# A pool of its own for the map's chunks, and six more places for gathered rows instead of four

## The chip, the cores and the metric

One core of one Trainium2 chip runs the whole program. The time is device microseconds (us) of one execution; shown are the median and the extremes of several. Everything is float32 in and out.

## The reference, cut to what matters

The kernel computes one decoder layer for 512 tokens of width 1024: mixing (attention and retention), then the expert retrieval `peer`, then a gate and a norm. The change concerns `peer`. Each token picks 8 x 16 = 128 of 16,384 experts; an expert is one row of `u` and one row of `v` (1024 floats each):

```
def peer(m, w_query, sub_keys, u, v):
    ...
    expert = jnp.take_along_axis(cand_idx, top_pos, axis=-1)
    gates = jax.nn.softmax(top_s, axis=-1)
    ...
    def chunk(args):
        xt, e, g = args
        u_sel = jnp.take(u, e, axis=0)
        act = jax.nn.gelu(jnp.einsum('cd,ced->ce', xt, u_sel).astype(jnp.float32), approximate=False) * g
        v_sel = jnp.take(v, e, axis=0)
        return jnp.einsum('ce,ced->cd', act.astype(xt.dtype), v_sel)
```

## The kernel before

The 512 tokens are four blocks of 128. The kernel treats them in two ways.

**The dense way (blocks 0 to 2, 384 tokens).** Every one of the 128 chunks of 128 experts is multiplied for all these tokens. A "u unit" is the product of one chunk of `u` with the tokens (24 matmuls into `ps`, line 85), after which ScalarE applies gelu. A "v unit" multiplies the weighted activations with one chunk of `v` and adds into six accumulators (18 matmuls into `acc`, line 781). Each unit's weights come as a 512 KB load `wraw` on SyncE's queue (lines 713, 719; `RAW` = 4 buffers), ScalarE makes the high part `wh` (line 745) and VectorE the low part `wl` (line 761). For a v unit VectorE also multiplies in the map (`av`, line 751), ScalarE rounds it to `ah` (line 754) and VectorE makes `al` (line 763). The weights of the experts chosen by each token are the "map": VectorE, TensorE and ScalarE build it in groups of 32 tokens. The chunks 0 to 23 (`KEEP`) stay in SBUF in the tile `kept`, 24 x 384 x 4 = 36,864 bytes of each partition; the other 104 go through a buffer `gs` (104 x 32 x 4 = 13,312 bytes, two of them) to DRAM (`g_d<-gs`, line 1137) and come back as `gv<-g_d` (line 726).

**The sparse way (block 3, 128 tokens).** For each of the 128 choices GpSimd gathers one row of `u` for each token, then one of `v`: 256 gathers of 128 rows x 4 KB (line 847, tile `row`). VectorE consumes each in a `sparse_step`: a dot product for `u` (line 858), a multiply-add into `yacc` for `v` (line 860). A gather can start only when its place is free, that is when the sparse step that read the place before is done. The pool `late` has three such places (`ROWS`). `gather()` is called after each sparse step and issues as many gathers as places are noted in `due`; a place of the pool `more` is given back only while `extra` is not empty.

**The order.** Each engine executes in the order in which the program writes its instructions. A first loop (lines 1183 to 1220) runs u units beside the building of the map. A second loop (lines 1370 to 1414) runs the rest of the u units, all v units and the last weights; it spreads the sparse steps by a table of costs. Sparse steps stand in VectorE's order between the instructions that make `wl` and `al`, so VectorE, waiting for a gathered row, also keeps back the operands of TensorE.

**The places in SBUF.** On the right side of SBUF pools open and close as a stack. `gsp` holds `kept` and the two `gs`. In the second loop `open_more` closes `gsp` and opens `more`, with `MORE` = 4 places, in its room; line 1391 allows that once the writes are issued (`not writes`) and the last unit that reads `kept` has been prepared (`prepared > last_kept`). 64 units before the end `open_fin` closes `more` and opens `fin`, the tiles of the last stage (`hs`, `pl`, `gl`, `gate_b`, `final_gain`), which SyncE's queue then loads.

Of the kernel before, what the change touches and what calls it, by code (L numbers as in the profile page):

```python
# [23 lines left out]
F32 = mybir.dt.float32  # L24
# [11 lines left out]
P = 128  # L36
# [4 lines left out]
ND = NT * P  # L41
# [13 lines left out]
def block_kernel(ctx: ExitStack, tc, t):  # L55
    nc = tc.nc

    def pool(name, bufs=1, **kw):
        return tc.tile_pool(name=name, bufs=bufs, reuse_waits="tile", **kw)
# [47 lines left out]
    def row_const(pool, name):  # L107

        r = pool.tile([P, D], F32, name=name)
        nc.sync.dma_start(r, row_src(name))  # L110
        return r
# [33 lines left out]
    with pool("wa", 2, side="right") as wa, pool("sm", 2, side="right") as sm, \  # L145
# [43 lines left out]
        def take():  # L189
            while steps[2] <= place[0]:  # L190
                cut_high()
                cut_low()
            place[0] += 1
            return cut_w.pop(place[0] - 1)
# [5 lines left out]
        def token_products(out, x, i):  # L200

            wh, wl = take()
            for k in range(2):
                xh, xl = x[2 * i + k]
                for b in range(4):
                    product3(out[b], [((xh[:, blk[b]], xl[:, blk[b]]), (wh[:, k], wl[:, k]))],
                             first=i + k == 0, last=i == 3 and k == 1)
            ahead()
# [4 lines left out]
        with pool("proj", side="right") as pj, pool("att", 2, side="right") as at:  # L213
# [276 lines left out]
            kept = []  # L490
# [202 lines left out]
        KEEP, RUN, QUAD = 24, 32, 4  # L693
# [12 lines left out]
        raw, parts, inputs, made, g_quad, kept_map = {}, {}, {}, {}, {}, []  # L706
# [107 lines left out]
        def spill(keep):  # L814

            while len(spills) > keep:
                nc.sync.dma_start(*spills.pop(0))

        vp, acc, count, done_u = [], [], [0], []
        writes, spills = [], []  # L820
# [12 lines left out]
        extra = {}  # L833
# [13 lines left out]
                nc.gpsimd.indirect_dma_start(out=rows[n], out_offset=None, in_=t[table],  # L847
                                             in_offset=bass.IndirectOffsetOnAxis(ap=e_sp[:, r:r + 1], axis=0))

        at_more, MORE = {}, 4  # L850

        def sparse_step():
            n = done[0]
# [13 lines left out]
        with pool("wp", 2, side="right") as wpp:  # L867
            hs = wpp.tile([P, 4, D], F32, name="hs", bufs=1)
            for b in range(4):
                nc.sync.dma_start(hs[:, b], t["x"][blk[b]])  # L870
            pT = wpp.tile([P, 2, S], F32, name="pT", bufs=1)
            nc.sync.dma_start(pT, t["pT"])
            gffn = row_const(wpp, "ffn_gain")
            ssm = sm.tile([P, 2, 4], F32, name="ssm", bufs=1)

            def add_mixing(half, ps):
                c = halves[half]
                for b in range(4):
                    nc.vector.tensor_tensor(hs[:, b, c], hs[:, b, c], ps[b], op=OP.add)
                    nc.scalar.activation(sqj[:, :S], hs[:, b, c], AF.Square, accum_out=ssm[:, half, b:b + 1])  # L880

            ps2 = [p.tile([P, S], F32, name="wo", tag=tag) for p, tag in ((psM, "misc"), (mm, "mm")) for _ in range(2)]
            token_products(ps2, cat, 0)
            add_mixing(0, ps)
            for i in range(1, 4):
                token_products(ps2, cat, i)
                if i == 1:
                    pH, pL = split(wpp, pT, [P, 2, S], "p", nc.vector, bufs=1)
                if i == 2:
                    for c in range(2):  # L890
                        load(("q", c))
                        prepare(("q", c), nc.vector)

            wh, wl = take()
            pp = [psS.tile([P, 2, S], F32, name="S", tag="S") for _ in range(2)]
            for b in range(4):
                product3(pp[b // 2][:, b % 2], [((pH[:, k, blk[b]], pL[:, k, blk[b]]), (wh[:, k], wl[:, k])) for k in range(2)])
            add_mixing(1, ps2)
            nc.sync.dma_start(h_d, hs)
            nc.vector.tensor_tensor(ssm[:, 0], ssm[:, 0], ssm[:, 1], op=OP.add)  # L900
            y = rstd(sm, ssm[:, 0], 4, D, 1e-6)
            mn = [wpp.tile([P, D], F32, name=f"mn{b}", bufs=1) for b in range(4)]
            for c in halves:
                for b in range(4):
                    if b % 2:
                        nc.vector.tensor_scalar(mn[b][:, c], hs[:, b, c], y[:, b:b + 1], None, op0=OP.mult)
                    else:
                        nc.scalar.activation(mn[b][:, c], hs[:, b, c], AF.Copy, scale=y[:, b:b + 1])
            mx = operand()
            for k in range(KC):  # L910
                pt = (psM, mm)[k % 2].tile([P, 4, P], F32, name="pt", tag=("misc", "mm")[k % 2])
                for b in range(4):
                    nc.tensor.transpose(pt[:, b], mn[b][:, k * P:(k + 1) * P], ident)
                scaled_split(*mx[k], pt.rearrange("p b t -> p (b t)"), gains[:, G_FFN, k:k + 1])
            kp = wpp.tile([P, 4, S], F32, name="kp", bufs=1)
            for b in range(2):
                nc.scalar.activation(kp[:, 2 * b:2 * b + 2], pp[b], AF.Copy)
            nc.sync.dma_start(ple_d[:, :, halves[1]], kp)
            nc.vector.tensor_tensor(mtok, mn[3], gffn, op=OP.mult)
    g_stack = ctx.enter_context(ExitStack())  # L920
    with pool("pk") as pk, pool("psG", 2, space=PSUM) as psG, pool("psT", space=PSUM) as psT:
        vals = pk.tile([P, 4, 16, TOPK], F32, name="vals")
# [20 lines left out]
        with pool("qs", 2) as qs:  # L943
            units = [("q", c) for c in range(16)] + [("u", n) for n in range(RAW - 1)]
            loaded, prepared = 2, 2
# [40 lines left out]
            rank(14)  # L986
            rank(15)

        gsp = g_stack.enter_context(pool("gsp", side="right"))
        kept_map.append(gsp.tile([P, KEEP, ND], F32, name="kept"))  # L990
        mh = pk.tile([P, ND], F16, name="mh")
        ml = pk.tile([P, ND], F16, name="ml")
        it = pk.tile([P, ND], BF16, name="it")
# [188 lines left out]
        n = 0  # L1182
# [50 lines left out]
    def open_fin():  # L1233

        extra.clear()
        while any(at_more.values()):
            sparse_step()
        more_stack.close()
        fin["p"] = fp = ctx.enter_context(pool("fin", 2, side="right"))
        for name, n in (("hs", 4), ("pl", 4)):  # L1240
            fin[name] = fp.tile([P, n, D], F32, name=name, bufs=1)
        fin["gl"] = fp.tile([P, KC, D], F32R, name="gl", bufs=1)
        for name in ("gate_b", "final_gain"):
            fin[name] = fp.tile([P, D], F32, name=name, bufs=1)
        fin["st"] = fp.tile([P, 8], F32, name="st", bufs=1)
# [66 lines left out]
    with pool("acc", space=PSUM) as pa:  # L1312
# [11 lines left out]
        n = 0  # L1324
# [19 lines left out]
        last_kept = max(n for n, u in enumerate(seq) if u[0] == "v" and u[1] < KEEP)  # L1344
# [3 lines left out]
        W_EVERY, END = 2, total - 64  # L1348
# [5 lines left out]
        writes = writes[2:]  # L1354
        prev = ("u", n_early - 1)
        loaded, prepared = RAW - 1, 2
# [13 lines left out]
        for n, u in enumerate(seq):  # L1370
            while loaded < min(total, n + RAW):
                kind, i = seq[loaded]
                if kind == "v" and i >= n_early and i not in late_a:
                    break
                assert kind != "v" or all((i - KEEP) // QUAD not in range(*x[1]) for x in writes)
                if kind == "g" and "gh" not in fin:
                    x = operand()
                    fin["gh"] = x
                load(seq[loaded])
                loaded += 1  # L1380
            while prepared < min(total, n + 3, loaded):
                prepare(seq[prepared], nc.vector)
                prepared += 1
            spill(0)
            finish(prev, prev[1] >= n_early)
            products(u)
            prev = u
            if writes and n % W_EVERY == 0:
                f, q, g = writes.pop(0)
                f(*q)  # L1390
            if not extra and n < END - 12 and not writes and prepared > last_kept:
                open_more()
            if n == END - 8:
                extra.clear()
            if n == END:
                open_fin()
            traffic += fixed[n]
            passed += busy_units[n]
            while done[0] < n_sp and (traffic + LOAD <= level * passed or n >= total - SPARSE_END):
                sparse_step()  # L1400
                gather()
                traffic += LOAD
            if 0 <= n - end_at < len(ends):
                name, b = ends[n - end_at]
                if b is None:
                    nc.sync.dma_start(fin[name], row_src(name))
                else:
                    nc.sync.dma_start(fin[name][:, b], sources[name][:, b])
            if n == total - 8:
                assert done[0] == n_sp  # L1410
                add_experts(3, [yacc[:, d * S:(d + 1) * S] for d in range(2)])
                fac[3] = rstd(fin["p"], fin["st"][:, 3:4], 1, D, 1e-6)
            if n == total - 2:
                turn(3, mm, "mm")
# [90 lines left out]
```

## Time and profile before

| | |
|---|---|
| median of 3 runs | 1603.94 us (1603.33 to 1609.25) |
| the profiled execution | 1605.48 us, of it span 1603.7 us |
| TensorE (PE) busy | 1542.4 us, 96% |
| VectorE (DVE) busy | 1222.3 us, 76% |
| ScalarE (ACT), GpSimd (POOL) busy | 678.9 us, 376.2 us |
| mean granted TensorE clock | 0.985 of full |
| moved by DMA | 402.72 MB, 251 GB/s on average |

TensorE is busy nearly all the time, so time can be found only where it stands still or runs slowly; the profile's table of stretches shows where. The page's chain of the work that ended last tells which wait holds TensorE up there. In the chain, "issue" is time in which an engine waited for nothing that the profile shows. The names of engines in the rows are PE (matmul), PEld (its weight load), DVE, ACT, POOL and SP.

### The profile page before, as it was taken

How to read it: one execution, taken by the hardware profiler on the slowest of the kernel's cores; microseconds unless marked ns; L12 is line 12 of the kernel's file. 1: busy time of each engine (PE TensorE's matmuls, PEld its weight loads, DVE VectorE, ACT ScalarE, POOL GpSimd, SP SyncE). 2: the span in 40 equal slices, each digit the busy share in tenths (PEclk: the TensorE clock that was granted, in tenths of full speed). 3: DMA queues.
4: the chain of work that ended last, by engine and by line, in shares of the span. 5: the costliest groups of instructions: out<-in, count | busy, mean ns of one | idle time of the engine just before them, and what ended most of it. 6: DMA issues, size and time to landing. Idle time of an engine off the chain costs nothing.

```text
span 1603.7 us, 22942 instructions
## 1 busy us (share of the span) xinstructions
PE 1542.4 (96%) x8209; PEld 1348.4 (84%) x8209; DVE 1222.3 (76%) x2523; ACT 678.9 (42%) x1077; POOL 376.2 (23%) x311
## 2 busy tenths in 40 slices
PE   8999999899999999999999898989999999999997
PEld 6787877787999999999999776777888888888885
DVE  3576565478998989998866787768888875897655
ACT  5455545444634453454343232323333333354444
POOL 1200000110013203203113444445434320432000
PEclk9899999999999999999999999999999999999998
DMA  6322324774458979987998888889999999899701
GB/s 230 102 76 79 112 99 185 213 176 117 167 187 268 319 219 316 297 283 259 315 295 305 307 301 306 308 288 343 408 386 366 359 328 346 302 401 345 255 28 48
DMA packets 163475, 402.72 MB, mean 251 GB/s; under 512 B 14528, under 2 KB 77259, under 8 KB 163233
## 3 DMA queue, kind: packets, MB, share of 16 engines
q1 hardware_dynamic: 123248, 256.06, 45.3%
q0 software_dynamic: 40112, 145.20, 27.2%
q8 instruction: 64, 1.05, 0.3%
q14 instruction: 51, 0.41, 0.1%
HBM read 350.61 MB, written 42.21 MB: 245 GB/s over the span
## 4 chain that ended last, share of the span: by engine, by line
PE 64%; DMA 13%; issue 11%; DVE 7%; POOL 2%; ACT 2%; SPq 0%; POOLq 0%; DVEq 0%; ACTq 0%
PE ps L85 32%; PE acc L781 19%; DMA row<-in_peer_v_dram,e_sp 7%; DMA row<-in_peer_u_dram,e_sp 4%; PE S L85 3%; POOL row L847 2%; PE S L322 1%; PE ps L517 1%; PE wo L85 1%; DVE wl L761 1%; PE pg L1116 1%; PE pg L1118 1%; DMA wraw<-in_u_t_dram 1%; PE sc L951 1%; DVE yacc L860 1%
## 5 line engine op out<-in xcount | busy, mean ns | idle before, releaser
L85 PE MATMUL ps<-xh,wh 128*128 128x384 f32 (+1 forms) x1312 | 466.4, 355 | 5.3 <-ACT kept L793 3.0
L85 PE MATMUL ps<-xh,wl 128*128 128x384 f32 (+1 forms) x1312 | 459.4, 350 | 7.3 <-DMA wl<-wraw 4.3
L85 PE MATMUL ps<-xl,wh 128*128 128x384 f32 (+1 forms) x1320 | 459.4, 348 | 0.0
L745 ACT ACTIVATE wh<-wraw 128x1024 fp32r<-128x1024 f32 x272 | 286.5, 1054 | 193.2 <-PE ps L85 101.8
L761 DVE TENSOR_TENSOR wl<-wraw,wh 128x1024 fp32r<-128x1024 f32 x258 | 314.6, 1221 | 64.7 <-ACT wh L745 60.0
L85 PEld LDWEIGHTS ps<-xh,wl 128*128 128x128 f32 x1312 | 248.6, 189 | 21.7 <-DMA wl<-wraw 4.8
L85 PEld LDWEIGHTS ps<-xh,wh 128*128 128x128 f32 x1312 | 249.1, 190 | 19.0 <-ACT kept L793 3.3
L847 POOL DMA_INDIRECT row<-in_peer_v_dram,e_sp x128 | 170.8, 1334 | 391.0 <-DVE act L858 309.6
L847 POOL DMA_INDIRECT row<-in_peer_u_dram,e_sp x128 | 169.1, 1321 | 387.4 <-DVE yacc L860 245.9
L85 PEld LDWEIGHTS ps<-xl,wh 128*128 128x128 f32 x1320 | 250.7, 190 | 10.7
L781 PE MATMUL acc<-wl,ah 128*128 128x512 f32 x768 | 240.2, 394 | 14.0 <-DVE wl L761 13.9
L781 PE MATMUL acc<-wh,ah 128*128 128x512 f32 x768 | 240.0, 394 | 9.6 <-ACT ah L754 9.4
L781 PE MATMUL acc<-wh,al 128*128 128x512 f32 x768 | 238.4, 392 | 0.0
L860 DVE SCALAR_TENSOR_TENSOR yacc<-row,act,yacc 128x1024 f32<-128x1024 f32 x128 | 163.9, 1280 | 30.6 <-DMA row<-in_peer_v_dram,e_sp 30.4
L781 PEld LDWEIGHTS acc<-wl,ah 128*128 128x128 f32 x768 | 143.8, 189 | 49.1 <-DVE wl L761 20.0
L858 DVE CUSTOM_DVE_ANT_0 junk<-row,mtok 128x1024 bf16<-128x1024 f32 x128 | 156.1, 1220 | 34.5 <-DMA row<-in_peer_u_dram,e_sp 34.1
L781 PEld LDWEIGHTS acc<-wh,ah 128*128 128x128 f32 x768 | 143.9, 189 | 44.4 <-ACT ah L754 15.6
L781 PEld LDWEIGHTS acc<-wh,al 128*128 128x128 f32 x768 | 143.8, 189 | 32.5 <-DVE al L763 3.2
L754 ACT ACTIVATE ah<-av 128x384 fp32r<-128x384 f32 x104 | 54.6, 525 | 255.0 <-PE acc L781 145.1
L1126 ACT ACTIVATE gs<-pg 128x832 f32<-128x832 f32 x48 | 41.5, 865 | 146.1 <-PE pg L1118 114.2
L763 DVE TENSOR_TENSOR al<-av,ah 128x384 fp32r<-128x384 f32 x104 | 57.7, 554 | 55.5 <-ACT ah L754 55.5
L185 DVE TENSOR_TENSOR wl<-wraw,wh 128x1024 fp32r<-128x1024 f32 x33 | 40.6, 1230 | 29.2 <-ACT wh L179 29.0
(288 smaller groups left out, 1711.6 us busy)
## 6 DMA issues: line engine op xcount, KB each, us to landing
wraw<-in_u_t_dram SPq DMA_DIRECT2D x128, 512.0 KB
wraw<-in_peer_v_dram SPq DMA_DIRECT2D x128, 512.0 KB
gv<-g_d SPq DMA_DIRECT2D x26, 768.0 KB
g_d<-gs SPq DMA_DIRECT2D x24, 576.0 KB
a<-av SPq DMA_DIRECT2D x72, 192.0 KB
av<-a SPq DMA_DIRECT2D x72, 192.0 KB
wraw<-in_w_in_t_dram SPq DMA_DIRECT2D x16, 512.0 KB
wraw<-in_wq_t_dram SPq DMA_DIRECT2D x16, 512.0 KB
```

Source lines behind the costliest of these rows:

```text
L85: nc.tensor.matmul(out, a, b, start=first and k == 0, stop=last and k == n - 1)
L185: nc.vector.tensor_tensor(cut_w[k][1], raw_w.pop(k), cut_w[k][0].bitcast(F32), op=OP.subtract)
L322: nc.tensor.matmul(out, *((a, b) if q_first else (b, a)), start=n == 0, stop=n == 1)
L745: nc.scalar.activation(wh, w, AF.Copy)
L754: nc.scalar.activation(ah, av, AF.Copy)
L761: low.tensor_tensor(wl, w, wh.bitcast(F32), op=OP.subtract)
L763: nc.vector.tensor_tensor(al, av, ah.bitcast(F32), op=OP.subtract)
L781: nc.tensor.matmul(acc[b][d], a[:, c], bb[:, d * S:(d + 1) * S], start=f, stop=l)
L847: nc.gpsimd.indirect_dma_start(out=rows[n], out_offset=None, in_=t[table], in_offset=bass.IndirectOffsetOnAxis(ap=e_sp[:, r:r + 1], axis=0))
L858: nc.vector.tensor_tensor_reduce(junk, row, mtok, 1.0, 0.0, OP.mult, OP.add, act[:, r:r + 1])
L860: nc.vector.scalar_tensor_tensor(yacc, row, act[:, r:r + 1], yacc, op0=OP.mult, op1=OP.add)
L1126: nc.scalar.activation(gs[0][:, :, t0:t0 + 8], pgi[:, KEEP:], AF.Copy, scale=2.0 ** -15)
```

## The change

`kept` moves from `gsp` into a pool of its own, opened just ahead of `gsp` on the same side. So `gsp` now holds only the two `gs`, and closing it no longer needs the readers of `kept` to be done. `open_more` may run as soon as no write is left to be issued; it opens 6 places (24,576 bytes) where the two `gs` (26,624 bytes) were. The pool of `kept` is closed in `open_fin`.

```
-        at_more, MORE = {}, 4
+        at_more, MORE = {}, 6
...
+    k_stack = ctx.enter_context(ExitStack())
     g_stack = ctx.enter_context(ExitStack())
...
+        kept_pool = k_stack.enter_context(pool("kept", side="right"))
+        kept_map.append(kept_pool.tile([P, KEEP, ND], F32, name="kept"))
         gsp = g_stack.enter_context(pool("gsp", side="right"))
-        kept_map.append(gsp.tile([P, KEEP, ND], F32, name="kept"))
...
         more_stack.close()
+        k_stack.close()
         fin["p"] = fp = ctx.enter_context(pool("fin", 2, side="right"))
...
-            if not extra and n < END - 12 and not writes and prepared > last_kept:
+            if not extra and n < END - 12 and not writes:
                 open_more()
```

On every engine the instructions stand in the same order as before; what differs is what some of them wait for. Numbering the gathers from 0, the first one into a place of `more` was gather 157; now it is gather 67. GpSimd's queue, with the semaphores that each gather waits for, before, from gather 65 on (`DMASW` counts GpSimd's transfers, `DMAHW` SyncE's, `DVE` and `Activation` those engines' instructions):

```order
L847 DMA row<-in_peer_v_dram,e_sp 128x1024 [waits DMASW0_49,DVE_49]
L847 DMA row<-in_peer_u_dram,e_sp 128x1024 [waits DMASW1_49,DVE_49]
L847 DMA row<-in_peer_v_dram,e_sp 128x1024 [waits DMASW2_49,DVE_49]
L847 DMA row<-in_peer_u_dram,e_sp 128x1024 [waits DMASW3_49,DVE_49]
L847 DMA row<-in_peer_v_dram,e_sp 128x1024 [waits DMASW4_49,DVE_49]
L847 DMA row<-in_peer_u_dram,e_sp 128x1024 [waits DMASW5_49,DVE_49]
L847 DMA row<-in_peer_v_dram,e_sp 128x1024 [waits DMASW6_49,DVE_49]
```

The same place now:

```order
L847 DMA row<-in_peer_v_dram,e_sp 128x1024 [waits DMASW0_49,DVE_49]
L847 DMA row<-in_peer_u_dram,e_sp 128x1024 [waits DMASW1_49,DVE_49]
L847 DMA row<-in_peer_v_dram,e_sp 128x1024 [waits DMAHW4_49,DMAHW3_49,DMAHW5_49,DMAHW2_49,DMAHW6_49,DMAHW1_49,DMAHW7_49,DMAHW0_49,Activation_49]
L847 DMA row<-in_peer_u_dram,e_sp 128x1024 [waits DMAHW5_49,DMAHW6_49,DMAHW4_49,DMAHW7_49,DMAHW3_49,Activation_49]
L847 DMA row<-in_peer_v_dram,e_sp 128x1024
L847 DMA row<-in_peer_u_dram,e_sp 128x1024
L847 DMA row<-in_peer_v_dram,e_sp 128x1024
L847 DMA row<-in_peer_u_dram,e_sp 128x1024 [waits DMASW2_49]
```

Gathers 67 and 68 wait for SyncE's transfers out of the two `gs` (and ScalarE's filling of them), gathers 69 to 72 for nothing that frees a place, and from gather 73 on each waits again for the sparse step that frees its place, which is now nine steps back instead of three.

A second place is SyncE's queue where `fin` opens. Before:

```order
L719 DMA wraw<-in_peer_v_dram 128x1024 [waits DMAHW4_49,DMAHW3_49,DVE_49]
L1408 DMA hs<-h_d 128x1024
L719 DMA wraw<-in_peer_v_dram 128x1024 [waits DMAHW7_49,DMAHW5_49,DVE_49]
L731 DMA av<-a_6497 128x384 [waits DMAHW6_49]
L1408 DMA hs<-h_d 128x1024
```

Now:

```order
L719 DMA wraw<-in_peer_v_dram 128x1024 [waits DMAHW4_49,DMAHW3_49,DVE_49]
L1411 DMA hs<-h_d 128x1024 [waits DMASW4_49,DMASW5_49,DMASW3_49,DMASW6_49,DMASW2_49,DMASW7_49,DMASW1_49,DMASW0_49]
L719 DMA wraw<-in_peer_v_dram 128x1024 [waits DMAHW7_49,DMAHW5_49,DVE_49]
L731 DMA av<-a_6500 128x384 [waits DMAHW6_49]
L1411 DMA hs<-h_d 128x1024
```

The first load of `hs` now waits for the gathers that used `more`, since `hs` lies partly where those places were; the loads of `final_gain` and `gate_b`, which waited for them before, no longer do.

## Rows read from the trace of the kernel before

**Rows 1.** Busy time of each engine by stretch: start:end, length, engines, clock, DMA share, GB/s

```profile
600.00:700.00 100.00, 100.00 (x733) 97.64 (x732) 91.88 (x179) 42.22 (x58) 26.74 (x20) 1.00 0.91 307
...
851.00:1110.00 259.00, 233.80 (x1069) 193.27 (x1068) 196.06 (x245) 80.03 (x113) 121.01 (x90) 0.99 0.86 307
1110.00:1160.00 50.00, 50.00 (x236) 44.03 (x237) 44.69 (x58) 17.35 (x23) 29.78 (x23) 0.97 1.00 392
1160.00:1290.00 130.00, 130.00 (x597) 110.47 (x597) 110.81 (x148) 47.64 (x66) 48.62 (x40) 1.00 0.97 366
...
1070.00:1080.00 10.00, 5.10 (x16) 3.82 (x15) 7.64 (x10) 2.63 (x5) 4.26 (x4) 0.83 0.73 257
```

**Rows 2.** The chain of waits, 840 to 1170 us: start, length, what

```profile
1063.51 9.71 DMA row<-in_peer_v_dram,e_sp
...
1077.61 4.39 DMA row<-in_peer_v_dram,e_sp
...
1109.84 30.02 PE acc L781 x124
1139.87 16.66 PE ps L85 x96
```

**Rows 3.** Who waited for whom, 851 to 1110 us: total us, times, longest

```profile
DVE junk L858 <- DMA row<-in_peer_u_dram,e_sp: 32.2, 22, 5.0
...
DVE yacc L860 <- DMA row<-in_peer_v_dram,e_sp: 26.0, 24, 3.2
PEld acc L781 <- DVE wl L761: 19.8, 20, 5.3
```

**Rows 4.** Stretches, matmuls into `acc` alone: length, busy (count), clock, DMA share, GB/s

```profile
851.00:1110.00 259.00, 170.10 (x705) 0.99 0.86 307
1110.00:1160.00 50.00, 33.50 (x140) 0.97 1.00 392
1160.00:1290.00 130.00, 113.50 (x501) 1.00 0.97 366
```

**Rows 5.** The same stretches, matmuls into `ps` alone

```profile
851.00:1110.00 259.00, 64.83 (x364) 0.99 0.86 307
1110.00:1160.00 50.00, 16.83 (x96) 0.97 1.00 392
1160.00:1290.00 130.00, 16.83 (x96) 1.00 0.97 366
```

**Rows 6.** GpSimd's queue in time: start, length, instruction, idle before and its releaser

```profile
851.01 0.94 POOL L847 DMA_INDIRECT row<-in_peer_v_dram,e_sp  x1 [23.78 <-DVE act L858]
...
1108.92 1.68 POOL L847 DMA_INDIRECT row<-in_peer_u_dram,e_sp  x1 [1.93 <-DMA av<-a]
...
1125.65 1.30 POOL L847 DMA_INDIRECT row<-in_peer_u_dram,e_sp  x1 [0.30 <-issue]
...
1291.34 0.94 POOL L847 DMA_INDIRECT row<-in_peer_v_dram,e_sp  x1 [2.46 <-DVE act L858]
```

**Rows 7.** SyncE's queue in time, the last writes of the map and a load of `hs`

```profile
833.34 2.56 SPq L1137 DMA_DIRECT2D g_d<-gs  x3
...
1306.74 0.43 SPq L1408 DMA_DIRECT2D hs<-h_d  x1
```

**Rows 8.** Who waited for whom, 1110 to 1290 us

```profile
DVE al L763 <- ACT ah L754: 15.1, 19, 1.8
...
DVE wl L761 <- ACT wh L745: 7.8, 9, 1.6
...
ACT wh L745 <- DMA wraw<-in_u_t_dram: 2.7, 2, 2.3
...
DVE yacc L860 <- DMA row<-in_peer_v_dram,e_sp: 0.8, 1, 0.8
```

**Rows 9.** Who waited for whom, SyncE's queue alone, 830 to 1110 us

```profile
SPq L719 <- DVE wl L761: 178.4, 41, 9.6
SPq L713 <- DVE wl L761: 56.7, 14, 7.7
```

## The prediction

> **What bounds the kernel now.** I read the table of stretches first, since TensorE is the engine that is nearly full. From 600 to 700 us and from 1110 to 1290 us it stands still for nothing; from 851 to 1110 us it is busy for 233.8 of 259 us [rows 1]. So that stretch, the first of the second loop, is where something else sets the pace. The chain of waits says what: between 851 and 1109 us it is made of gathers, "DMA row" 23 times with 4.39 to 9.71 us each (the shortest and the longest are shown), joined by GpSimd's issues and VectorE's steps; from 1109.84 us on it is matmuls, 30.02 us in a row [rows 2]. A loop of three places goes round: a sparse step frees a place, GpSimd issues a gather into it, the gather lands 4 to 10 us later, and VectorE, which has used up the two others, waits. It does so for 32.2 + 26.0 = 58.2 us there, and TensorE's weight load waits for VectorE's `wl` [rows 3]. The change of pace comes at 1108.92 us, when gather 157 starts a run of gathers without a wait for a free place [rows 6]: that is the moment when the four more places open.
>
> What TensorE loses in the stretch is more than its idle time, because a matmul that waits or that runs at the lower clock counts as busy. So I count matmuls at the pace of 1160 to 1290 us, where nothing is lost: 113.50 / 501 = 0.2265 us for one into `acc`, 16.83 / 96 = 0.1753 us for one into `ps` [rows 4, 5]. The stretch holds 705 and 364 of them: 705 x 0.2265 + 364 x 0.1753 = 159.7 + 63.8 = **223.5 us of work in 259 us, so 35.5 us are lost**. Of these 259 - 233.8 = 25.2 us are idle; part of the rest is clock: in two slices of 10 us, of which one is shown, and in the 50 us after 1110 us, the granted clock falls to 0.83 and 0.97 after TensorE stood still [rows 1], so it spent some 3 us at 1.2 instead of 2.4 GHz each time. The 50 us behind the stretch hold 140 x 0.2265 + 96 x 0.1753 = 48.5 us of work [rows 4, 5]: another 1.5 us lost. All in all 37 us are there to be had at most.
>
> **The change, part by part.** No instruction is added, removed or moved on any engine.
>
> *The earlier opening.* Gather 67 no longer waits for a sparse step but for the transfers of the map out of `gs`, and behind it on GpSimd's queue stand all later gathers. The last three writes are issued within 833.34 + 2.56 = 835.9 us [rows 7]. When they land no row shows; taking the gathers' 4.39 to 9.71 us for it [rows 2], they land at 840 to 846 us, against 851.01 us at which gather 67 is issued now [rows 6]. So the new wait ends 5 to 11 us before the old one did, and costs nothing; it would begin to cost when the writes took over 15 us. Eleven gathers at the old opening were issued from 1108.92 to 1125.65 us, 1.67 us apart [rows 6]; six at that pace are out by 857 us. From then on nine places go round instead of three.
>
> *What goes.* With nine places a gather may take six sparse steps longer to land. The 90 or so gathers of the stretch come 259 / 90 = 2.9 us apart now and would come 223.5 / 90 = 2.5 us apart, so each has about 20 us to land, twice the longest of [rows 2]. With the seven places of the next stretch VectorE waited for rows for 0.8 us in 180 us [rows 8]. I take the 58.2 us as gone.
>
> *What is late next.* Three candidates. TensorE: 223.5 us. VectorE: 196.1 us busy plus 259 - 196.1 - 58.2 = 4.7 us of other gaps, 201 us; from above, with waits for ScalarE at the share that they have from 1110 to 1290 us (15.1 + 7.8 of 180 us, 12.7% [rows 8]) it is 196.1 / 0.873 = 225 us. It carried 92% in a stretch in which TensorE never stood still [rows 1] and would carry 88% here; it is no bound, or one just equal to TensorE's. DMA: the stretch moves 307 GB/s x 259 us = 79.5 MB, and six gathers of 128 x 4 KB = 0.52 MB come into it from later: 82.6 MB, in 223.5 us 370 GB/s. The next stretches carried 392 GB/s for 50 us and 366 GB/s for 130 us, with TensorE full [rows 1]. So DMA is close, and I take 366 GB/s, the nearest row with the same kind of work: 82.6 / 0.366 = 226 us, a gain of 33 us. From below I take 350 GB/s: 236 us, 23 us; from above no limit, 37 us. The Trainium skill (DMA: Bandwidth & Descriptors, Specifications) gives some 358 GB/s as a core's share of HBM, which would make it 231 us, a gain of 28 us. The row of 392 GB/s speaks against it as a ceiling for one core alone, and I give it no weight.
>
> *The opening itself.* Six gathers, 3.1 MB, come at once where the first `wraw` loads of v units start. At the old opening the same happened with eleven gathers and the 50 us lost 1.5 us [rows 1, 4, 5]. I take off 2 us.
>
> *The end.* The first load of `hs` gets a wait for the gathers that used `more`; behind it on SyncE's queue stand the `wraw` loads. It is issued at 1306.74 us [rows 7], the last gather that can have used such a place at 1291.34 us or before [rows 6]; with 9.71 us to land [rows 2] it is there by 1301. It costs nothing; were each landing doubled, about 4 us on a queue whose loads run ahead by four units of 4 us. The other two waits that go there were as idle.
>
> *After 1110 us* TensorE is full already, and two places more bring nothing: 0.
>
> **Sum:** 33 - 2 = 31 us. The profiled execution takes 1605.48 us: 1574.5. It lies 1.5 us over the median of 1603.94, so the forecast for the median is **1573 us**, and its own range goes from a gain of 37 to one of 23: 1567 to 1581.
>
> **The rivals.**
> A, *DMA gives less than that.* The stretch has DMA's share at 0.86 [rows 1], which may be engines held up by something other than the ring: then gathers just land later, and the rate rises from 307 only part of the way, to 315 to 345 GB/s, say. For: 0.86 is not far from 1. Against: 392 GB/s in the next 50 us, in the same kernel with the same loads. At 330 GB/s the stretch takes 82.6 / 0.330 = 250 us: a gain of 9, less 2 for the opening: 1597; the case covers 1581 to 1598.
> B, *nothing changes.* Either the rate stays at 307 GB/s, or gather 67 and all behind it wait so long for the writes that the ring stays at three. The first would lengthen the stretch by 3.1 / 0.307 = 10 us, which come back behind 1110 us, where these gathers need no longer be made. 1604. Against: the run of eleven gathers at 1.67 us [rows 6] and the landing of the writes, for which there are 15 us.
> C, *slower: the weights come late.* With up to nine gathers outstanding instead of three, `wraw` loads wait behind them in DMA; ScalarE's `wh`, VectorE's `wl` and TensorE follow. The price: the stretch has 705 / 18 + 364 / 24 = 54 units, so that each us by which a unit's weights are late costs 54 us, and from 0.66 us on it eats the 35.5 us; at 1 us the time is 1604 - 35 + 54 = 1623. It decides from the point at which a load takes longer than its lead. A load is issued when VectorE's `wl` of four units before is done: SyncE's queue waits 178.4 + 56.7 us for nothing but that [rows 9]. Four units are 4 x 223.5 / 54 = 16.5 us, less some 3 us for `wh` and `wl`: about 13 us, more than the longest landing of a gather now. Against: from 1110 to 1290 us, with seven places and 366 to 392 GB/s, ScalarE waited for `wraw` for 2.7 us in all [rows 8].
>
> **How the numbers follow.** Forecast (gain 23 to 37 us): 0.74. A: 0.13. B: 0.07. C: 0.06. The range of 8 in 10 takes in the forecast's own, 1567 to 1581, one us below it, and half of A, down to a gain of 16 us: 1566 to 1588. A measurement of this kernel can tell about 0.5% from no change, 8 us: faster than 1596 is the forecast and nearly all of A, 0.86; the same 0.08; slower 0.06.
>
> **What the profile after would show.** Right: gather 67 at 840 to 851 us with five more about 1.7 us apart behind it; VectorE's waits for rows in the stretch under 10 us instead of 58.2; TensorE at 98% or more from 851 us until the 705 and 364 matmuls are done, at about 1077 to 1080; the chain made of matmuls there; DMA at about 365 GB/s and a share near 0.97; the stretch behind it unchanged in length. A would show VectorE still waiting for rows, with longer landings, at a DMA share near 1. B would show the first gather into `more` late, or the rate at 307. C would show ScalarE's `wh` waiting for `wraw`. I would be wrong above all if the rate of 366 to 392 GB/s is the working off of a backlog that this stretch can't have, or if VectorE's gaps grow with its load so that it, not TensorE, sets the pace at over 230 us.

## The result, and the profile after

The changed kernel takes 1566.76 us (median of 4 runs, 1565.33 to 1569.92) against 1604.12 us of the kernel before (4 runs). The ratio is 0.9766, with a 95% interval of 0.9743 to 0.9788: 37 us less. The forecast was 1573 us in a range of 1566 to 1588; the measured time lies at the low end of that range, 0.24 us under the 1567 us to which the forecast's own case went.

The profiled execution after has a span of 1564.5 us, 39.2 us shorter. The last writes of the map are issued 1.9 us earlier than in [rows 7], which is ahead of the change's first effect, so some 37 us come from the change. The stretches of the profile after, to be read against [rows 1]: nearly as many `acc` and `ps` matmuls as filled 851 to 1110 us now fill 851 to 1073 us, so the stretch behind it starts 37 us earlier (start:end, length, PE, PEld, DVE, ACT, POOL, clock, DMA share, GB/s):

```profile
851.00:1073.00 222.00, 222.00 (x1063) 194.20 (x1062) 198.45 (x251) 80.89 (x113) 129.18 (x90) 1.00 0.97 364
...
1073.00:1123.00 50.00, 50.00 (x244) 44.23 (x244) 42.77 (x56) 17.84 (x24) 23.24 (x18) 1.00 1.01 387
```

TensorE is busy for all of the 222 us, at the full clock. The counts behind it, for `acc` and then for `ps` alone:

```profile
851.00:1073.00 222.00, 161.52 (x710) 1.00 0.97 364
...
851.00:1073.00 222.00, 61.61 (x353) 1.00 0.97 364
```

At the full pace of [rows 4, 5] these are 710 x 0.2265 + 353 x 0.1753 = 222.7 us of work: nothing is lost any more. The chain of waits from 840 to 1170 us, where "DMA row" stood in [rows 2], has matmuls and nothing else (start, length, what; the first pieces behind the opening):

```profile
862.13 24.52 PE acc L781 x108
886.65 16.66 PE ps L85 x96
...
```

Who waited for whom from 851 to 1073 us: VectorE's waits for rows, 58.2 us in [rows 3], have no line; what is left are waits for ScalarE, which itself waits for TensorE:

```profile
ACT ah L754 <- PE acc L781: 76.3, 30, 2.8
...
DVE al L763 <- ACT ah L754: 14.7, 14, 1.9
...
DVE wl L761 <- ACT wh L745: 7.9, 11, 1.8
```

The opening on GpSimd's queue (start, length, instruction, idle before and its releaser), gathers 67, 68 and 72:

```profile
824.82 0.94 POOL L847 DMA_INDIRECT row<-in_peer_v_dram,e_sp  x1 [0.30 <-ACT gs L1128]
840.84 0.94 POOL L847 DMA_INDIRECT row<-in_peer_u_dram,e_sp  x1 [15.08 <-DMA g_d<-gs]
...
846.75 1.73 POOL L847 DMA_INDIRECT row<-in_peer_u_dram,e_sp  x1 [0.30 <-issue]
```

Gather 67 goes at once, without a wait for a transfer out of `gs`; gather 68 waits 15.08 us for the last writes, which the profile has issued from 831.42 us on. All six are out by 848.5 us.

### The profile page after: what moved, and what is told of

The parts are those of the page before. It is cut to its first block, busy times and chain, and to the rows that moved or that the text cites. A ratio compares the mean times of both kernels' runs of the same rounds, so it can differ in the third digit from the quotient of the medians.

```text
span 1564.5 us, 22940 instructions
## 1 busy us (share of the span) xinstructions
PE 1525.8 (98%) x8209; PEld 1346.2 (86%) x8209; DVE 1220.9 (78%) x2523; ACT 680.2 (43%) x1077; POOL 384.2 (25%) x311
## 4 chain that ended last, share of the span: by engine, by line
PE 88%; DVE 5%; DMA 3%; ACT 2%; issue 1%; SPq 0%; POOL 0%; ACTq 0%; DVEq 0%; POOLq 0%
PE ps L85 42%; PE acc L781 33%; PE S L85 3%; PE S L322 1%; PE ps L517 1%; PE pg L1118 1%; PE pg L1120 1%; PE wo L85 1%; DVE wl L761 1%; PE sc L952 1%; PE po L457 1%; DMA wraw<-in_w_val_dram 1%; PE po L638 1%; DMA row<-in_peer_v_dram,e_sp 1%; DMA row<-in_peer_u_dram,e_sp 1%
## 5 line engine op out<-in xcount | busy, mean ns | idle before, releaser
L847 POOL DMA_INDIRECT row<-in_peer_u_dram,e_sp x128 | 174.9, 1366 | 392.1 <-DVE yacc L860 241.9
L85 PEld LDWEIGHTS ps<-xl,wh 128*128 128x128 f32 x1320 | 249.5, 189 | 10.6
L781 PE MATMUL acc<-wh,ah 128*128 128x512 f32 x768 | 236.7, 389 | 0.8 <-ACT ah L754 0.8
L781 PE MATMUL acc<-wl,ah 128*128 128x512 f32 x768 | 236.6, 389 | 0.0
```

The source lines that it names most:

```text
L85: nc.tensor.matmul(out, a, b, start=first and k == 0, stop=last and k == n - 1)
L781: nc.tensor.matmul(acc[b][d], a[:, c], bb[:, d * S:(d + 1) * S], start=f, stop=l)
```

## The experiments

The theory: in the first stretch of the second loop the places for rows go round too slowly; three are too few, and the number of places that go round there is all that the change mends. Against it: that the sixth place or the other places in SBUF matter, that DMA's rate is the bound, and that each place brings an even part.

**Four places instead of six, opened early.**

```
-        at_more, MORE = {}, 6
+        at_more, MORE = {}, 4
```

> The changed kernel with 4 places in the early pool instead of 6, so that seven go round from 851 us on instead of nine. Ring theory (the number of places in the first stretch of the second loop set its length, and three were too few): at one gather in 2.5 us seven places leave 17 us for a landing, against 4 to 10 us seen; TensorE stays full, 1567 us, at most 3 us off. Rival (each added place brings its part of the gain): 37 us for six places, 6 us each, so 12 us slower, 1579 us.

Measured: 1568.28 us, ratio to the kernel before 0.9778 (0.9748 to 0.9807). Within the noise of the changed kernel; VectorE waits for no row in the stretch. So the two added places have no part that can be seen.

**The old condition, six places.**

```
-            if not extra and n < END - 12 and not writes:
+            if not extra and n < END - 12 and not writes and prepared > last_kept:
```

> The changed kernel with the old condition for opening (the last reader of the kept chunks must be prepared): the separate pool and the six places stay, only the early opening goes. Ring theory: 1604 us, within 3 us of the kernel before, VectorE's waits for rows in the first stretch back at about 58 us. Rival (the places in SBUF, or nine places instead of seven later on, carry part of the gain): 1570 to 1595 us.

Measured: 1605.6 us, ratio 1.0005 (0.9987 to 1.0022), no difference. The waits for rows from 851 to 1110 us are those of [rows 3] again:

```profile
DVE junk L858 <- DMA row<-in_peer_u_dram,e_sp: 34.8, 23, 5.2
DVE yacc L860 <- DMA row<-in_peer_v_dram,e_sp: 26.7, 22, 3.0
```

The separate pool, the new places of `fin` and nine places after 1110 us are worth nothing; the whole gain hangs on the moment of the opening.

**One place and two places, opened early.** The edit is that of the first run with `MORE` = 1 and 2.

> The changed kernel with a single place in the early pool: four go round instead of three. Ring theory: three places went round in 3 x 2.9 = 8.7 us; four at the same speed allow one gather in 2.2 us, less than the 2.5 us wanted, so that most of the gain is there already and what is left is bunches of sparse steps: 1570 to 1583 us, and VectorE's waits for rows 10 to 25 us in the stretch. Rival (each added place brings its part): 6 us of gain, 1598 us. Rival (DMA's rate in the stretch is what counts and more gathers under way only land later): 1600 us or more with landings of about 12 us.

> The early pool with 2 places: five go round. With one place the time was 1580 us, with four 1568 us. Ring theory: five places at 8.7 us a round allow a gather in 1.7 us, well under the 2.5 us wanted, and what is left is bunching: 1569 to 1574 us. A theory in which the gain falls off evenly with the places: 1576 us.

Measured: 1579.7 us with one place (ratio 0.9835, 0.9802 to 0.9868) and 1567.99 us with two (0.9768, 0.9742 to 0.9794). VectorE's waits for rows, with one place (851 to 1110 us) and with two (851 to 1090 us):

```profile
DVE junk L858 <- DMA row<-in_peer_u_dram,e_sp: 15.5, 18, 2.2
DVE yacc L860 <- DMA row<-in_peer_v_dram,e_sp: 13.6, 13, 3.2
```

```profile
DVE yacc L860 <- DMA row<-in_peer_v_dram,e_sp: 3.0, 5, 1.3
DVE junk L858 <- DMA row<-in_peer_u_dram,e_sp: 2.1, 2, 1.8
```

With one place the waits are 29.1 us, more than the 10 to 25 us expected; the time lies in its range. The rival in which more gathers under way only land later expected landings of about 12 us; the median was 7.5 us.

All in one table, with the places that go round in that stretch and the median landing of its gathers from 851 to 1073 us (the kernel before and the changed kernel have none on record; for three places it is that of the run with the old condition):

| places | VectorE's waits for rows, us | median landing, us | time, us |
|---|---|---|---|
| 3 (kernel before) | 58.2 | 6.4 | 1604 |
| 4 | 29.1 | 7.5 | 1580 |
| 5 | 5.1 | 7.8 | 1568 |
| 7 | none | 8.0 | 1568 |
| 9 (changed kernel) | none | not on record | 1567 |

The first place brings 24 us, the second 12, the rest nothing that can be told from noise. This is a ring that is too short, not a gain that is shared out evenly; with two places the run came out 1 us under the 1569 to 1574 us that the theory gave it. The landings do get longer with more places, but by less than the added places give.

**Half the bytes with three places.** Two ways to shorten the landing instead of adding places, both on the kernel before. First, rows for 64 of the 128 tokens (the main lines of the edit):

```
...
-                nc.gpsimd.indirect_dma_start(out=rows[n], out_offset=None, in_=t[table],
-                                             in_offset=bass.IndirectOffsetOnAxis(ap=e_sp[:, r:r + 1], axis=0))
+                nc.gpsimd.indirect_dma_start(out=rows[n][:64], out_offset=None, in_=t[table],
+                                             in_offset=bass.IndirectOffsetOnAxis(ap=e_sp[:64, r:r + 1], axis=0))
...
-                nc.vector.tensor_tensor_reduce(junk, row, mtok, 1.0, 0.0, OP.mult, OP.add, act[:, r:r + 1])
+                nc.vector.tensor_tensor_reduce(junk[:64], row[:64], mtok[:64], 1.0, 0.0, OP.mult, OP.add, act[:64, r:r + 1])
...
```

> The kernel before, with every gather fetching the rows of 64 tokens instead of 128 and the sparse steps working on those 64 (the other 64 tokens get no expert output): the number of gathers, steps, places and waits stays, the bytes of a gather are halved. Ring theory (time to land times places): a landing falls from a median of 7.4 us to some 4 to 5 us, three places go round in about 6 us, one gather in 2 us, and the stretch loses little: 1570 to 1580 us. Rival (a fixed cost of issuing and finishing makes up the landing): landings stay above 6.5 us, 1595 us or more.

Measured: 1603.93 us, ratio 0.999 (0.9968 to 1.0011). A miss: nothing was gained, as the rival had it. VectorE still waits for rows, 29.1 + 27.0 us from 851 to 1110 us. Then half a row, 512 floats, for each of the 128 tokens (the main lines):

```
...
-                nc.gpsimd.indirect_dma_start(out=rows[n], out_offset=None, in_=t[table],
+                nc.gpsimd.indirect_dma_start(out=rows[n], out_offset=None, in_=t[table].rearrange("e (z t) -> (e z) t", t=S),
...
-            row = rows.pop(n)
+            row = rows.pop(n)[:, None, :].to_broadcast([P, 2, S])
...
```

> The kernel before, with gathers for all 128 tokens but only 512 of the 1024 floats of a row (each half is then used twice, so VectorE's instructions keep their size; the expert output is not the reference's): half the bytes, spread over all partitions, which the run with 64 tokens did not do. Bytes theory (a landing is mostly bytes waiting their turn among 16 engines): the median landing falls from 7.4 to about 5 us, three places go round in about 6.5 us, 1570 to 1585 us. Fixed-cost theory (issue and completion make up most of it): landings of 6.5 to 7 us again, 1595 us or more.

Measured: 1565.61 us, ratio 0.9753 (0.973 to 0.9776): with three places as before, the whole gain, and more than the 1570 to 1585 us expected. The rows of the two runs from 851 to 1073 us, the 64 tokens first: GpSimd's queue of DMA (packets, MB, share of 16 engines) and the time from issue to landing of the gathers:

```profile
q0 software_dynamic: 6263, 20.55, 35.8%
...
DMA to landing us min/median/max: 3.7/5.5/9.2
```

```profile
q0 software_dynamic: 6980, 22.89, 31.1%
...
DMA to landing us min/median/max: 3.3/4.8/8.6
```

The fall in the landing was smaller for the 64 tokens than expected. The 7.4 us of the expectations is the median of the landings in the chain of the kernel before, that is, of the gathers that held VectorE up; all gathers of three places with whole rows, from the run with the old condition and the same stretch, have a median of 6.4 us:

```profile
DMA to landing us min/median/max: 4.1/6.4/11.5
```

So 64 tokens took 0.9 us off the landing and half rows 1.6 us. In the same 222 us the 64 tokens had 79 gathers, one in 2.8 us, against 77 of the kernel before, one in 2.9 us; half rows had 89, one in 2.5 us. A fixed cost that makes up the landing, which the first of the two runs still allowed, is ruled out by the second: it would have kept the landings at 6.5 to 7 us.

What follows: a shorter landing does the same as more places, so it is the time of a round that counts, and neither the number of bytes as such nor VectorE or TensorE. The round has to fit into three times 2.5 us, 7.5 us: with a median landing of 4.8 us it just does (VectorE waits 22.4 us for rows, which TensorE does not feel), with 5.5 us it does not. Why 64 tokens gained so little is only partly shown: their gathers held the engines for 35.8 / 20.55 = 1.74% of the stretch per MB, those of half rows for 31.1 / 22.89 = 1.36%, so that half the bytes in this form were far from half the work. For one gather this is 35.8 / 79 = 0.45% and 31.1 / 89 = 0.35%, and 51.6 / 77 = 0.67% in the kernel before. The Trainium skill (SBUF — State Buffer, Door 1: The DMA port swizzle) says that partitions 0 to 63 reach only 8 of SBUF's 16 DMA ports, which goes the same way; that the ports are the cause was not tried.

**Added loads, to find DMA's ceiling.** The early opening with four places, and one load per unit that nothing reads, as long as `kept` is in use (the edit for 128 KB; for 256 KB the 256 columns become 512):

```
+            if extra and prepared <= last_kept:
+                d = extra["p"].tile([P, 256], F32, name="dum", tag="dum", bufs=2)
+                nc.sync.dma_start(d, t["peer_v"][(n % P) * P:(n % P + 1) * P, :256])
```

> The early opening with 4 places, and in the first stretch one added load of 128 KB that nothing reads per unit on SyncE's queue, 53 of them, 6.9 MB: 89.5 MB would have to go in 222 us, 403 GB/s. If DMA's ceiling is about 400 GB/s: 224 us, within 5 us of the run without the loads, 1568 to 1573 us. If it is at the 366 GB/s at which the prediction capped the stretch: 89.5 / 0.368 = 243 us, 1589 us.

> The same with 256 KB per unit, 13.9 MB: 96.5 MB, 435 GB/s in 222 us. Ceiling about 400 GB/s: 241 us, 19 us slower than without, 1587 us, with DMA's share at 1.0 and waits for rows or weights back. Ceiling 366 GB/s: 262 us, 1608 us. No ceiling in reach: 1568 us.

Measured: 1568.12 us with 128 KB (ratio 0.9771, 0.9747 to 0.9795), as without; 1579.11 us with 256 KB (0.9839, 0.9814 to 0.9864), 11 us slower. The stretch, first with 128 KB, then with 256 KB:

```profile
851.00:1073.00 222.00, 222.00 (x1064) 194.35 (x1064) 198.03 (x251) 81.87 (x115) 129.18 (x90) 1.00 1.02 392
```

```profile
851.00:1073.00 222.00, 218.00 (x1035) 189.51 (x1033) 187.15 (x238) 78.37 (x110) 121.93 (x87) 0.99 1.03 402
```

392 GB/s cost TensorE nothing, so DMA's ceiling is not at 366 GB/s. 402 GB/s is the highest rate of this stretch in any run: DMA's share is 1.03, and of 40 slices of 5.55 us 36 run at 400 to 409 GB/s. The run with four places and no added loads has 361 x 222 = 80.1 MB in the stretch; with the 13.9 MB these are 94 MB, at 402 GB/s 234 us, 12 us more than 222, against the 11 measured. (The 19 us expected started from 82.6 MB without the added loads.) The changed kernel, at 364 GB/s, stands 10% under that.

How much of the 11 us is DMA's rate the run does not tell. The added loads have two buffers (`bufs=2`), so each waits on SyncE's queue for the last but one to land, and the weights' loads stand behind it. The queue's waits for that from 851 to 1073 us, with 128 KB and with 256 KB (total us, times, longest):

```profile
SPq L1398 <- DMA dum<-in_peer_v_dram: 96.6, 38, 7.4
```

```profile
SPq L1398 <- DMA dum<-in_peer_v_dram: 173.0, 51, 6.8
```

With 256 KB the queue hardly ever waits for VectorE's `wl` any more (2.9 us, against 147.3 + 46.6 us in the run with four places and no added loads), and 67% of the chain of waits from 851 to 1090 us are added loads:

```profile
846.02 7.33 DMA dum<-in_peer_v_dram
...
853.41 8.09 DMA dum<-in_peer_v_dram
```

Two buffers with a median landing of 8.1 us let one load go in some 4.1 us, which is just the 222 / 54 = 4.1 us of a unit. So a ring that is too short and DMA engines that are full stand side by side, and the two cannot be told apart here; added loads with more buffers were not tried. What TensorE feels is late weights, as in the prediction's rival C, and not a wait for rows; with 256 KB, from 851 to 1090 us:

```profile
ACT wh L745 <- DMA wraw<-in_peer_v_dram: 86.6, 38, 3.7
```

The `wraw` loads of v units landed in a median of 9.4 us with 128 KB and of 10.6 us with 256 KB.

## Why the prediction was right, point by point

**The place and the cause** were right: a ring of three places in the stretch from 851 to 1110 us. The old condition alone takes back the whole gain, and each added place takes away VectorE's waits, as do shorter landings.

**The work and the loss** were right: 222.7 us of matmuls now fill 222 us, and the loss of 35.5 us, with the 1.5 us behind it, is gone to the last us. The count of matmuls at full pace was the better measure: TensorE's idle time alone would have given 25 us. The clock was part of it: the 50 us behind the stretch had 0.97 [rows 1] and now have 1.00.

**What is late next** was where the sum was off. The forecast took DMA to be the next bound, at the 366 GB/s of the stretch behind, and so gave away 35.5 - 33 = 2.5 us. Two things were wrong there. That row showed what was asked for, not what could be had: with added loads the stretch ran at 392 GB/s without loss, so the row of 392 GB/s, which stood beside it, was the right one. And the stretch had less to move than the 82.6 MB: the six gathers that were to come into it were all issued ahead of 851 us, the stretch holds 90 gathers as before, and at 364 GB/s it moved 80.8 MB. Even at 366 GB/s these take 221 us, no more than TensorE's matmuls. The Trainium skill's 358 GB/s (DMA: Bandwidth & Descriptors, Specifications) is not the limit here either: 402 GB/s were measured on one core alone. VectorE is as near to being a bound as was said (198.45 us busy, its waits for ScalarE 14.7 + 7.9 us, together 221 of 222 us), but those waits follow TensorE.

**The opening** was taken to cost 2 us and cost nothing: from 840 to 851 us, while the six gathers came, DMA moved 408 GB/s and TensorE was busy for all of the 11 us. The 2 us had been read from the 1.5 us lost behind the old opening, which the prediction also counted among the losses to be had; they are gone with the stalls ahead of them. The 2.5 us and the 2 us, and the 1.5 us of slow clock behind the stretch that the sum left out, are the 6 us between the forecast's gain of 31 and the measured 37. So the mechanism was right and the sum too cautious: the measured time stands where the prediction had put the lower limit of its own case, with all of the loss gone.

**The added wait** was right in kind: the last writes land at 840.8 us, in the 840 to 846 us that were taken from the gathers' landings. But it is gather 68 that waits for them, not 67, which was issued at 824.82 us, ahead of the 840 to 851 us that were said. The 15.08 us cost nothing: in the kernel before GpSimd issued no gather in that time either, but sat idle for 23.78 us up to 851.01 us [rows 6].

**The end**: the wait of the first `hs` load costs nothing. It is issued at 1267.09 us against 1306.74 us [rows 7], 39.65 us earlier, as everything behind the stretch, and from 1250 to 1300 us SyncE's queue waits for VectorE alone.

**The rivals.** A (DMA gives less) and B (nothing changes) fell with the result. C (late weights) did not come with 392 GB/s and did with 256 KB of added loads per unit. Whether the 13 us of lead were right is not shown by that: there the weights' loads were not issued four units ahead but held on SyncE's queue behind the added loads.

## What to carry to other kernels

A ring of buffers needs at least as many places as the time of one round, from free place to consumed data, holds of the steps that the bound engine allows: here 8.7 / 2.5 = 3.5, so four. That is the mean, and it is not quite enough: four still lost 12 us, five did it, and the four after that brought nothing. What the fifth place is for was not separated: the landings themselves grew from 6.4 to 8.0 us as places were added, and the sparse steps may come in bunches. When a buffer's room is held back by a neighbour in the same pool that lives longer, a pool of its own for the neighbour costs nothing and can open the room much earlier, here by some 270 us. To tell a bound by transfer rate from a ring that is too short, look for the best rate in any stretch of the same kernel, and if in doubt add loads that nothing reads until it hurts; but give them buffers enough, or they are a short ring of their own. And compare landings of all gathers with landings of all gathers: those in the chain of waits are the late ones.

## What the runs showed of the hardware that was not expected

One core's DMA engines carried up to 402 GB/s over 222 us, with a share of 1.03 in the profile's count; up to 392 GB/s TensorE felt nothing. Gathers into 64 partitions held the engines 1.74% of the stretch per MB where gathers of half rows into 128 partitions held them 1.36%, and 64 tokens' gathers landed in 5.5 us against 4.8 us: halving the tokens brought no time at all, halving the rows 39 us. From 1123 to 1253 us, with seven places, 64 tokens' gathers had DMA's share at 1.04 with only 270 GB/s moved, half rows at 0.80 with 275 GB/s.
